# A recurrent unit's elimination matrix fetched through DRAM, and its outputs summed in one PSUM bank

## The chip, the core and the metric

The kernel runs on one core of one Trainium2 chip. The metric is the device time of one launch in microseconds. Engines are named as in the profile: PE (TensorE matmul), PEld (its weight loads), DVE (VectorE), ACT (ScalarE), POOL (GpSimd) and SP, whose queue issues every DMA of this kernel.

## The reference

Two layers of a hybrid block run on 256 latent and 256 context tokens of width 2048. Each layer normalises, projects with `w_in`, runs three branches on the projection's columns (grouped-query attention, a bidirectional RWKV-7 scan, pooling), concatenates and projects with `w_out`. What the change touches is the RWKV branch: 8 heads of size 64, one scan in each direction.

```python
def step(S, inp):
    r_t, w_t, k_t, v_t, kk_t, a_t = inp
    sa = jnp.einsum('bhvk,bhk->bhv', S, kk_t)
    S = S * w_t[:, :, None, :] - sa[..., None] * (kk_t * a_t)[:, :, None, :] + v_t[..., None] * k_t[:, :, None, :]
    return S, jnp.einsum('bhvk,bhk->bhv', S, r_t)
```

The outputs of both directions are added, normalised per head, and gated. Layer 1 needs no output for the context tokens.

## The kernel before, in words

**The main stream.** Weights arrive as 256 KB tiles `wf`; ACT casts each to a rounded high part and DVE subtracts it from the tile (`w_split`, lines 1099 to 1116, tiles `sp`); PE multiplies high and low parts with the activations' parts `h` into PSUM tiles `acc` (`main_in`, `main_out`).

**The recurrent units.** In each layer 8 units, each a pair of heads (group `g`, 0 to 3) by a stream of 256 tokens (`s`, context or latent), are cut into 4 chunks of 64 tokens. Of the 16 units 12 need outputs (`need`): 8 in layer 0, 4 in layer 1. A unit passes through workers that hand it on by queues:

- `front` (line 1297) loads r, k, v, normalises k into `kk`, and makes the factors `W` and `BK` of both directions.
- `back` (line 1413) multiplies them on PE and masks the products on DVE into `UB` and `W`. Then it copies the 32x32 diagonal blocks of the triangular matrices into a tile `N0` (lines 1444 to 1448, eight ACT copies).
- `elim` (line 1457) inverts those blocks. Two DVE transposes (lines 1460 to 1463) spread `N0` into `DT`, the only tile of its class, and 31 steps of one product and one sum each follow on DVE (lines 1469 to 1475), in a chain. Four small transposes give the inverse in two orders, `T1` and `T2`.
- `fin` (line 1486) joins 32-blocks to 64-blocks with copies on ACT and small matmuls.
- `scan` (line 1526) takes 4 steps, in each chunk `i` forward and chunk `3-i` backward. A step's outputs are accumulated by 8 matmuls in a PSUM tile `psO`, which DVE copies or adds into an SBUF tile `OT` (lines 1594 to 1600). After the last step `OT` is normalised (lines 1604 to 1614) and transposed back.

**What sets the order.** The kernel is a program that plans itself: workers yield instructions, and `Scheduler.run` (lines 544 to 625) emits them one by one by a model of the engines, by the time at which each could start and its worker's priority. Every engine then runs its instructions strictly in the order emitted, and waits on semaphores for what they need. A DMA's price in the plan is

```python
            if op.eng == "D":
                self.free_at["D"] = s + 60
                st = max(self.dma_free, s + 60)
                self.dma_free = st + op.dur / 350.0
                end = self.dma_free + DMA_LATENCY
```

with `op.dur` its bytes and `DMA_LATENCY` 2900, all in ns (line 203, lines 589 to 593). `HELD` (line 208, used in line 572) is added to the start of a DVE or ACT instruction whose partitions begin elsewhere than those of the one before it.

**PSUM** has 8 banks of 128x512; tiles of class `scan` may hold up to 3, and 2 are kept for them.

## Time and profile before

| what | value |
|---|---|
| three runs | 1724.2, 1725.89 (median), 1728.25 us |
| profiled execution, its own time | 1729.24 us |
| span of its trace, first to last instruction | 1727.4 us |
| mean granted clock of PE | 0.987 |
| DMA | 349.77 MB, mean 202 GB/s |

The profile lists busy time by engine and by stretch, groups of instructions with a mean duration and the idle time ahead of them, what each engine waited for, the DMAs, and the chain of work that ended last, followed back from the end. A busy PE is not a PE at its peak: matmuls overlap, and a group's mean is the time that one takes from start to end, not the distance between two. Nearly all instructions are emitted by one line, 588, where the planner calls them, so groups are told apart by their tiles: `tp<-dt,tp` is written to a tile `tp` from tiles `dt` and `tp`.

In the span the stretch from 216 to 720 us holds the recurrent units of layer 0, from 720 to 1080 us there are none, and from 1080 to 1620 us those of layer 1.

### The profile page before, as it was taken

What the parts mean: (1) busy time and instruction counts of PE and PEld (TensorE: products, weight loads), DVE (VectorE), ACT (ScalarE), POOL (GpSimd) and SP (SyncE); (2) the same over time, 40 slices, a digit from 0 to 9 for tenths busy, and PEclk for the clock granted to TensorE, in tenths of its full rate; (3) what the DMA queues carried; (4) which work ended last, traced back from release to release, by engine and by line L of the source; (5) the groups of instructions that cost most, each with busy time, mean ns of one, the idle gap of its engine ahead of it and who ended that gap; (6) DMA issues with size and microseconds to landing.
All of it is one profiled execution on the core that took longest, in us unless ns stands there. A gap on an engine that the chain in (4) does not pass through costs nothing.

```text
span 1727.4 us, 38237 instructions
## 1 busy us (share of the span) xinstructions
PE 1657.9 (96%) x13658; PEld 1336.4 (77%) x13658; DVE 1348.7 (78%) x4250; ACT 929.0 (54%) x2279; POOL 9.3 (1%) x77
## 2 busy tenths in 40 slices
PE   4899999999999999999999999989999999999997
PEld 3677676776777777777777889789999988998885
DVE  4335889898898898854557685899999999999663
ACT  5333454544555555534346574666546757766461
POOL 0000000000000000000000000000000000000000
PEclk9999999999999999999999999999999999999998
DMA  9993763567566655568579964574523554564762
GB/s 330 374 364 104 248 198 102 178 205 230 162 190 184 218 186 182 178 205 297 193 238 361 331 214 156 160 259 142 160 87 125 167 152 150 178 186 151 259 199 98
DMA packets 217822, 349.77 MB, mean 202 GB/s; under 512 B 22880, under 2 KB 61856, under 8 KB 217632
## 3 DMA queue, kind: packets, MB, share of 16 engines
q1 hardware_dynamic: 217632, 347.34, 61.4%
q8 instruction: 107, 1.75, 0.4%
q14 instruction: 83, 0.68, 0.1%
HBM read 316.41 MB, written 30.83 MB: 201 GB/s over the span
## 4 chain that ended last, share of the span: by engine, by line
PE 76%; DVE 10%; DMA 9%; ACT 2%; issue 2%; SPq 1%; DVEq 0%; ACTq 0%
PE acc L588 54%; PE pr L588 6%; PE att L588 6%; PE scan L588 5%; PE ada L588 4%; DVE tp L588 3%; DMA wa<-in_ada_w_dram 2%; DVE sp L588 2%; DMA w<-in_ada_w_dram 2%; DMA wf<-in_w_in_dram 2%; DVE rf L588 1%; DMA pw<-in_w_in_dram 1%; DVE dt L588 1%; PE st L588 1%; SPq L588 1%
## 5 line engine op out<-in xcount | busy, mean ns | idle before, releaser
L588 PE MATMUL acc<-h,sp 128*128 128x256 f32 (+1 forms) x5088 | 971.2, 339 | 11.4 <-DVE h L588 4.3
L588 PEld LDWEIGHTS acc<-h,sp 128*128 128x128 f32 x5088 | 759.1, 189 | 124.9 <-issue 11.6
L588 DVE TENSOR_TENSOR sp<-wf,sp 128x512 fp32r<-128x512 f32 (+1 forms) x568 | 359.4, 661 | 38.0 <-ACT sp L588 31.9
L588 ACT CAST sp<-wf 128x512 fp32r<-128x512 f32 (+1 forms) x624 | 351.3, 604 | 21.5 <-PE acc L588 5.7
L588 PE MATMUL acc<-sp,h 128*128 128x512 f32 x1152 | 278.4, 398 | 0.1
L588 PEld LDWEIGHTS acc<-sp,h 128*128 128x128 f32 x1152 | 215.0, 189 | 50.1 <-DVE sp L588 1.0
L588 DVE TENSOR_TENSOR tp<-tp 128x60 f32<-128x60 f32 (+21 forms) x552 | 134.4, 246 | 7.1 <-ACT tp L588 0.3
L588 DVE TENSOR_TENSOR tp<-dt,tp 128x48 f32<-128x48 f32 (+23 forms) x496 | 111.0, 224 | 6.3
L588 PEld LDWEIGHTS scan<-rf 128*64 128x64 f32 x1344 | 57.2, 138 | 34.6 <-issue 9.5
L588 PE MATMUL scan<-rf 128*64 128x64 f32 x1344 | 78.0, 233 | 1.7 <-DVE rf L588 1.0
L588 PE MATMUL ada<-wa,cs 128*2 128x256 f32 x1024 | 71.9, 378 | 2.5 <-DMA wa<-in_ada_w_dram 2.2
L588 ACT CAST pw<-pw 128x512 fp32r<-128x512 f32 x56 | 34.8, 622 | 65.4 <-DMA pw<-in_w_in_dram 59.8
L588 DVE TENSOR_TENSOR rf<-tp 64x256 f32<-64x256 f32 x176 | 69.2, 419 | 0.2
L588 DVE STREAM_TRANSPOSE dt<-tp 128x1024 f32<-128x1024 f32 x32 | 65.8, 2075 | 0.1
L588 DVE TENSOR_TENSOR pw<-pw 128x512 f32<-128x512 f32 x56 | 38.4, 686 | 34.5 <-ACT pw L588 34.2
L588 ACT ACTIVATE aq<-att,q 128x512 f32<-128x512 f32 (+1 forms) x48 | 34.0, 708 | 57.0 <-DVE q L588 40.7
L588 DVE COPY adasb<-ada 2x128 f32<-2x128 f32 (+1 forms) x32 | 11.4, 357 | 66.0 <-ACT adasb L588 63.9
L588 DVE SCALAR_TENSOR_TENSOR q<-q 128x4 f32<-128x4 f32 (+3 forms) x378 | 56.9, 155 | 3.7
L588 PE MATMUL ada<-w,cs 128*2 128x128 f32 x1024 | 37.5, 295 | 21.2 <-DMA w<-in_ada_w_dram 20.2
L588 ACT COPY rf<-scan 64x128 f32<-64x128 f32 x128 | 33.3, 260 | 44.1 <-PE scan L588 40.6
L588 ACT COPY adasb<-ada 2x128 f32<-2x128 f32 (+1 forms) x32 | 9.9, 309 | 87.2 <-PE ada L588 83.7
L588 ACT COPY sm<-scan 128x128 f32<-128x128 f32 x64 | 17.1, 267 | 69.6 <-PE scan L588 69.1
(153 smaller groups left out, 1936.6 us busy)
## 6 DMA issues: line engine op xcount, KB each, us to landing
wf<-in_w_in_dram SPq DMA_DIRECT2D x384, 256.0 KB, 3.6
wa<-in_ada_w_dram SPq DMA_DIRECT2D x256, 256.0 KB, 4.6
wf<-in_w_out_dram SPq DMA_DIRECT2D x192, 256.0 KB, 4.7
w<-in_ada_w_dram SPq DMA_DIRECT2D x128, 256.0 KB, 5.4
pw<-in_w_in_dram SPq DMA_DIRECT2D x56, 256.0 KB, 4.5
w<-pw SPq DMA_DIRECT2D x56, 256.0 KB, 2.5
sp<-w SPq DMA_DIRECT2D x56, 256.0 KB, 3.5
wf<-in_w_in_dram SPq DMA_DIRECT2D x48, 128.0 KB, 4.6
```

The lines of the kernel that those rows point to most:

```text
L588: op.call(**op.args)
```

## The change

It has four parts. First, `kk` is made from `k` directly: ACT's Square takes the scale `rw_k_k`, a `scalar_tensor_tensor` takes it too, and the separate product `kr` is gone. Second, `N0` and the two transposes into `DT` are gone: `back` writes the blocks from `UB` to a DRAM scratch `nd` (4 of them in turn) with 8 DMAs of 16 KB, in runs of 128 B, and `elim` reads them into `DT` with 16 DMAs of 64 KB, each of which repeats 8 KB to 8 partitions. Both directions now lie in `DT` in the same order, so the steps of `elim` address the two directions with access patterns built by hand, and `T1` and `T2` change roles for direction 1. Third, `psO` is one PSUM bank for all 4 steps of a unit, with a column range for each chunk; the copies and sums into `OT` are gone, and the normalisation reads the bank. Fourth, `HELD` is 120.25 in place of 121.75.

```diff
--- before.py
+++ after.py
@@ -205,7 +205,7 @@
 WHOLE = (128, 128)
 SWITCH = 95.0
 BACK = 60.0
-HELD = 121.75
+HELD = 120.25
 HOLD = {None: 1000.0, "ada": 3000.0}
 PRIO = {"setup": 6, "start": 6, "scan": 5, "front": 3, "back": 4, "elim": 4, "fin": 4, "evac": 4, "pre": 4, "gate": 4, "att": 4, "rg": 5, "mix": 5, "load": 1, "ada": 3, "wl": 2, "ws": 6, "main": 0, "norm": 6, "turn": 3, "post": 6}
 
@@ -646,6 +646,7 @@
         self.ahead = AHEAD_OF()
         self.low = {w: [dram("w%d_%d" % (n, i), [128, 512]) for i in range(2)] for n, w in enumerate(self.ahead)}
         self.ygd = [dram("ygd%d" % l, [4, 128, 512]) for l in range(DEPTH)]
+        self.nd = [dram("nd%d" % i, [4, 2, 4, 32, 32]) for i in range(4)]
         self.sch = Scheduler(tiles, CLASSES, log)
         self.sch.set_phase(PHASES["start"])
         self.flags = set()
@@ -1310,15 +1311,13 @@
             yield D_.dma_start(out=rkv[j], in_=self.rkvd[l][j, g, :, cs])
         r, k, v = rkv
 
-        kr = yield Alloc("tp", (128, 256))
-        yield V.tensor_scalar(out=kr, in0=k, scalar1=self.vec(l, "rw_k_k", g), scalar2=None, op0=ALU.mult)
         sq = yield Alloc("tp", (128, 256))
-        yield S.activation(out=sq, in_=kr, func=AF.Square)
+        yield S.activation(out=sq, in_=k, func=AF.Square, scale=self.vec(l, "rw_k_k", g))
         psb = yield from self.norm_bc(sq, self.k("hones"), 1.0, 1e-24, ALU.max, "pr")
         self.free(sq)
         kk = yield Alloc("tp", (128, 256))
-        yield V.tensor_tensor(out=kk, in0=kr, in1=psb[:, 0:256], op=ALU.mult)
-        self.free(kr, psb)
+        yield V.scalar_tensor_tensor(out=kk, in0=k, scalar=self.vec(l, "rw_k_k", g), in1=psb[:, 0:256], op0=ALU.mult, op1=ALU.mult)
+        self.free(psb)
 
         BK, W = [], [[], []]
         yield Until(lambda: len(self.fq) == 0)
@@ -1441,38 +1440,41 @@
                 yield V.tensor_tensor(out=W[p][d][H[1 - p], 0:nj].rearrange("p j c t -> p c j t"),
                                       in0=pa[H[1 - p], :, 0:nj, :], in1=mk(H[1 - p]), op=ALU.mult)
                 self.free(psA[p])
-        N0 = yield Alloc("tp", (128, 2, 4, 32))
-        for q in range(4):
-            b = q % 2
-            for d in range(2):
-                yield S.copy(out=N0[Q[q], d], in_=UB[d][Q[q], :, 0, 32 * b:32 * b + 32])
+        nd = self.nd[self.count.setdefault("nd", 0) % len(self.nd)]
+        self.count["nd"] += 1
+        for d in range(2):
+            for q in range(4):
+                b = q % 2
+                yield D_.dma_start(out=nd[q, d].rearrange("c s t -> s c t"), in_=UB[d][Q[q], :, 0, 32 * b:32 * b + 32])
         for d in range(2):
             psW = yield Alloc("pr", (128, 512))
             for c in range(4):
                 yield T.transpose(out=psW[:, 128 * c:128 * c + 128], in_=BK[d][:, c].rearrange("p a b -> p (a b)"), identity=ident)
             yield S.copy(out=BK[d].rearrange("p c h k -> p (c h k)"), in_=psW)
             self.free(psW)
-        self.push(self.bq, (N0, (l, g, s, need, RS, W, UB, BK, PC, bv)))
-
-    def elim(self, N0, unit):
+        self.push(self.bq, (nd, (l, g, s, need, RS, W, UB, BK, PC, bv)))
+
+    def elim(self, nd, unit):
         V = self.V
         DT = yield Alloc("dt", (128, 2, 32, 32))
-        for d in range(2):
-            src = N0[:, d].rearrange("p c t -> p t c").unsqueeze(2).to_broadcast([128, 32, 8, 4])
-            dst = DT[:, 0].rearrange("p a b -> p b a") if d == 0 else DT[:, 1]
-            yield V.transpose(out=dst, in_=src)
-        self.free(N0)
+        for q in range(4):
+            for c in range(4):
+                src = nd[q, :, c].rearrange("d s t -> d (s t)").unsqueeze(0).to_broadcast([8, 2, 1024])
+                yield self.D.dma_start(out=DT[32 * q + c:32 * q + 32:4].rearrange("p d s t -> p d (s t)"), in_=src)
         ZZ = yield Alloc("tp", (128, 2, 32, 4))
         TM = yield Alloc("tp", (128, 256))
         z0 = self.k("z0").rearrange("p (a m) -> p a m", m=4).unsqueeze(1).to_broadcast([128, 2, 32, 4])
         yield V.tensor_copy(out=ZZ, in_=z0)
+        grid = lambda x, o, *dims: bass.AP(x.tensor, x.offset + o, [list(x.ap[0])] + [list(n) for n in dims])
         for t in range(31, 0, -1):
-            m0 = t // 8
+            r, m0 = 31 - t, t // 8
             M = 4 - m0
             tm = TM[:, 0:2 * t * M].rearrange("p (d a m) -> p d a m", d=2, a=t)
-            yield V.tensor_tensor(out=tm, in0=DT[:, :, 0:t, t:t + 1].to_broadcast([128, 2, t, M]),
-                                  in1=ZZ[:, :, t:t + 1, m0:4].to_broadcast([128, 2, t, M]), op=ALU.mult)
-            yield V.tensor_tensor(out=ZZ[:, :, 0:t, m0:4], in0=ZZ[:, :, 0:t, m0:4], in1=tm, op=ALU.add)
+            n = grid(DT, t, (1024 + 32 * (r + 1) + r - t, 2), (32, t), (0, M))
+            row = grid(ZZ, 4 * t + m0, (128 + 4 * r - 4 * t - m0, 2), (0, t), (1, M))
+            z = grid(ZZ, m0, (128 + 4 * (r + 1) - m0, 2), (4, t), (1, M))
+            yield V.tensor_tensor(out=tm, in0=n, in1=row, op=ALU.mult)
+            yield V.tensor_tensor(out=z, in0=z, in1=tm, op=ALU.add)
         self.free(DT, TM)
         T1 = yield Alloc("tp", (128, 2, 32, 4))
         T2 = yield Alloc("tp", (128, 2, 4, 32))
@@ -1488,14 +1490,14 @@
         for q in range(4):
             b = q % 2
             yield S.copy(out=UB[0][Q[q], :, 0, 32 * b:32 * b + 32], in_=T1[Q[q], 0].rearrange("p c u -> p u c"))
-            yield S.copy(out=UB[1][Q[q], :, 0, 32 * b:32 * b + 32], in_=T2[Q[q], 1])
+            yield S.copy(out=UB[1][Q[q], :, 0, 32 * b:32 * b + 32], in_=T1[Q[q], 1].rearrange("p c u -> p u c"))
         psY = yield Alloc("pr", (128, 512))
         for u in range(4):
             for p in range(2):
                 q0, q1 = Q[2 * p], Q[2 * p + 1]
                 o = slice(32 * u, 32 * u + 32)
                 yield T.matmul(out=psY[q1, o], lhsT=UB[0][q0, u, 0, 32:64], rhs=T2[q0, 0, u, :], start=True, stop=True)
-                yield T.matmul(out=psY[q0, o], lhsT=UB[1][q1, u, 0, 0:32], rhs=T1[q1, 1, :, u], start=True, stop=True)
+                yield T.matmul(out=psY[q0, o], lhsT=UB[1][q1, u, 0, 0:32], rhs=T2[q1, 1, u, :], start=True, stop=True)
         YS = yield Alloc("tp", (128, 4, 32))
         yield S.copy(out=YS.rearrange("p u t -> p (u t)"), in_=psY[:, 0:128])
         self.free(psY)
@@ -1505,7 +1507,7 @@
                 q0, q1 = Q[2 * p], Q[2 * p + 1]
                 o = slice(32 * u, 32 * u + 32)
                 yield T.matmul(out=psZ[q0, o], lhsT=YS[q1, u, :], rhs=T1[q1, 0, :, u], start=True, stop=True)
-                yield T.matmul(out=psZ[q1, o], lhsT=YS[q0, u, :], rhs=T2[q0, 1, u, :], start=True, stop=True)
+                yield T.matmul(out=psZ[q1, o], lhsT=YS[q0, u, :], rhs=T1[q0, 1, :, u], start=True, stop=True)
         psz3 = psZ[:, 0:128].rearrange("p (u t) -> p u t", u=4)
         for p in range(2):
             yield S.copy(out=UB[0][Q[2 * p], :, 0, 32:64], in_=psz3[Q[2 * p]])
@@ -1526,9 +1528,8 @@
     def scan(self, Sc, l, g, s, need, RS, W, UB, W2, PC, bv):
         V, S, G, T, D_ = self.V, self.S, self.G, self.T, self.D
         ident = self.k("ident")
-        OT = None
         if need:
-            OT = yield Alloc("ts", (128, 4, 64))
+            psO = yield Alloc("scan", (128, 512))
         if s == 1:
             for p in range(2):
                 yield V.tensor_copy(out=RS[H[p], p, 0:4:3, :], in_=Sc[H[p]])
@@ -1546,11 +1547,10 @@
             yield S.copy(out=X, in_=psX[:, 0:128])
             self.free(psX)
             if need:
-                psO = yield Alloc("scan", (128, 512))
                 for d in range(2):
                     for p in range(2):
-                        yield T.matmul(out=psO[H[p], 64 * d:64 * d + 64], lhsT=W[p][d][:, 1, c[d], :], rhs=RS[:, p, c[d], :],
-                                       start=(d == 0), stop=False, skip_group_check=True)
+                        yield T.matmul(out=psO[H[p], 64 * c[d]:64 * c[d] + 64], lhsT=W[p][d][:, 1, c[d], :], rhs=RS[:, p, c[d], :],
+                                       start=(i == 0 and d == 0), stop=False, skip_group_check=True)
             psS = yield Alloc("scan", (128, 512))
             for d in range(2):
                 for p in range(2):
@@ -1569,8 +1569,8 @@
             if need:
                 for d in range(2):
                     for p in range(2):
-                        yield T.matmul(out=psO[H[p], 64 * d:64 * d + 64], lhsT=UB[d][H[p], c[d], 1, :], rhs=RS[H[p], p, c[d], :],
-                                       start=False, stop=(d == 1), skip_group_check=True)
+                        yield T.matmul(out=psO[H[p], 64 * c[d]:64 * c[d] + 64], lhsT=UB[d][H[p], c[d], 1, :], rhs=RS[H[p], p, c[d], :],
+                                       start=False, stop=(i == 3 and d == 1), skip_group_check=True)
             if not last:
                 sm = yield Alloc("sm", (128, 2, 64))
                 pn3 = psN[:, 0:128].rearrange("p (d v) -> p d v", d=2)
@@ -1591,20 +1591,16 @@
             else:
                 self.free(Sc)
                 Sc = None
-            if need:
-                po = psO[:, 0:128].rearrange("p (d v) -> p d v", d=2)
-                if i < 2:
-                    yield V.tensor_copy(out=both(OT, c), in_=po)
-                else:
-                    yield V.tensor_tensor(out=both(OT, c), in0=both(OT, c), in1=po, op=ALU.add)
-                self.free(psO)
         self.free(RS, *W[0], *W[1], *UB, *W2, PC)
         if need:
             st = yield Alloc("q", (128, 4))
-            yield V.tensor_reduce(out=st, in_=OT, axis=AX.X, op=ALU.add)
+            O4 = psO[:, 0:256].rearrange("p (c v) -> p c v", c=4)
+            yield V.tensor_reduce(out=st, in_=O4, axis=AX.X, op=ALU.add)
             yield V.tensor_scalar(out=st, in0=st, scalar1=1.0 / 64, scalar2=None, op0=ALU.mult)
             bc = lambda ap: ap.unsqueeze(2).to_broadcast([128, 4, 64])
-            yield V.tensor_tensor(out=OT, in0=OT, in1=bc(st), op=ALU.subtract)
+            OT = yield Alloc("ts", (128, 4, 64))
+            yield V.tensor_tensor(out=OT, in0=O4, in1=bc(st), op=ALU.subtract)
+            self.free(psO)
             sq = yield Alloc("ts", (128, 4, 64))
             yield S.activation(out=sq, in_=OT, func=AF.Square)
             yield V.tensor_reduce(out=st, in_=sq, axis=AX.X, op=ALU.add)
```

## Rows read from the trace of the kernel before

**Rows 1.** The profile page: busy time and share of each engine.

```profile
PE 1657.9 (96%) x13658; PEld 1336.4 (77%) x13658; DVE 1348.7 (78%) x4250; ACT 929.0 (54%) x2279; POOL 9.3 (1%) x77
```

**Rows 2.** Stretches: from:to us, length; busy PE, PEld, DVE, ACT, POOL; clock, DMA share, GB/s.

```profile
216.00:720.00 504.00, 495.89 (x4287) 362.78 (x4286) 455.97 (x1577) 264.42 (x689) 3.81 (x34) 1.00 0.58 185
720.00:1080.00 360.00, 357.41 (x2125) 283.40 (x2124) 223.28 (x509) 186.34 (x399) 0.61 (x4) 1.00 0.74 246
1080.00:1620.00 540.00, 529.76 (x5066) 482.03 (x5065) 501.24 (x1708) 347.45 (x892) 3.53 (x28) 0.99 0.51 163
```

**Rows 3.** Waits of PE from 216 to 1620 us: total us, times, longest.

```profile
PE acc L588 <- DMA sp<-w: 2.3, 2, 1.1
PE ada L588 <- DMA wa<-in_ada_w_dram: 2.2, 4, 0.7
PE acc L588 <- DVE sp L588: 2.1, 4, 1.1
```

**Rows 4.** Chain that ended last: whole run, 216:720 us, 1080:1620 us.

```profile
PE 76%; DVE 10%; DMA 9%; ACT 2%; issue 2%; SPq 1%; DVEq 0%; ACTq 0%
...
by line: PE acc L588 32.3%; PE scan L588 8.7%; PE pr L588 8.4%; PE att L588 8.1%; DVE tp L588 6.8%; PE ada L588 6.6%; DMA wa<-in_ada_w_dram 5.0%; DVE sp L588 4.3%; issue 3.7%; DVE rf L588 3.1%; DVE dt L588 2.1%; DMA rkvd<-ev 1.4%; DVE q L58
...
by line: PE acc L588 58.2%; PE pr L588 9.6%; PE scan L588 7.4%; PE att L588 6.6%; DVE tp L588 3.0%; DMA wf<-in_w_in_dram 2.0%; DMA sp<-w 1.5%; DVE sp L588 1.4%; DVE dt L588 1.3%; DMA x1d<-y 1.1%; issue 1.0%; DVE q L588 0.9%; DVE rf L588 0.8
```

**Rows 5.** One piece of that chain, in order of time: start, us, what.

```profile
949.11 58.03 PE acc L588 x248
```

**Rows 6.** Groups of instructions by shape: count, busy us, mean ns, idle before.

```profile
L588 PE MATMUL acc<-sp,h 128*128 128x512 f32 x1152 | 278.4, 398 | 0.1
...
L588 DVE STREAM_TRANSPOSE dt<-tp 128x1024 f32<-128x1024 f32 x32 | 65.8, 2075 | 0.1
...
L588 ACT COPY tp<-rb 32x128 f32<-32x128 f32 x128 | 37.6, 295 | 20.0 <-DVE rb L588 18.2
...
L588 ACT ACTIVATE tp<-tp 128x256 f32<-128x256 f32 x80 | 30.4, 413 | 30.1 <-DVE tp L588 27.7 <-DVE q L588 1.9
...
L588 DVE TENSOR_REDUCE q<-ts 128x4 f32<-128x256 f32 x24 | 9.8, 409 | 0.1
...
L588 DVE COPY ts<-scan 128x128 f32<-128x128 f32 x24 | 6.8, 281 | 0.7 <-PE scan L588 0.4
L588 DVE TENSOR_TENSOR ts<-ts,scan 128x128 f32<-128x128 f32 x24 | 6.7, 281 | 0.1
...
L588 DVE TENSOR_REDUCE q<-att 128x1 f32<-128x256 f32 x16 | 6.7, 416 | 2.4 <-PE att L588 2.4
...
L588 DVE TENSOR_TENSOR tp<-tp,pr 128x256 f32<-128x256 f32 x16 | 6.6, 414 | 3.1 <-PE pr L588 2.9
...
L588 DVE SCALAR_TENSOR_TENSOR tp<-tp,hk 128x256 f32<-128x256 f32 x12 | 5.7, 476 | 0.0
...
L588 DVE TENSOR_SCALAR tp<-tp,vecs 128x256 f32<-128x256 f32 x16 | 5.5, 342 | 0.6 <-DMA tp<-rkvd 0.6
...
L588 ACT ACTIVATE at<-acc,vecs 128x256 f32<-128x256 f32 x8 | 3.8, 471 | 0.0
```

**Rows 7.** DMA issues on SP in order of time: start, us, what.

```profile
506.55 1.38 SPq L588 DMA_DIRECT2D tp<-rkvd  x3
...
511.43 1.75 SPq L588 DMA_DIRECT2D wa<-in_ada_w_dram  x4
```

**Rows 8.** DMA issues by tile: count, KB each, median us to landing.

```profile
tu<-in_rw_w_up_dram SPq DMA_DIRECT2D x16, 64.0 KB, 3.1
...
ta<-in_pool_w_dram SPq DMA_DIRECT2D x8, 64.0 KB, 4.3
...
gpd<-tl SPq DMA_DIRECT2D x2, 16.0 KB, 2.6
```

**Rows 9.** DVE from 1612 to 1616 us; the bracket is idle time before.

```profile
1613.21 0.48 DVE L588 SCALAR_TENSOR_TENSOR at<-y,vecs,at 128x256 f32<-128x256 f32 x1 [3.62 <-DMA y<-ygd]
```

**Rows 10.** PE in the same stretch.

```profile
1612.29 1.86 PE L588 MATMUL acc<-h,sp 128*128 128x256 f32 x13
```

## The prediction, made before the changed kernel ran

> **What bounds the kernel now.** I read the busy time of the whole run first. PE is busy for 96% of the span and DVE for 78% [rows 1]. By stretch the picture sharpens: while the recurrent units of layer 0 run, PE is busy 495.9 of 504 us and DVE 456.0, which is 90%; in layer 1 they stand at 529.8 and 501.2 of 540 us, so DVE reaches 93%. Between the two, DVE falls to 62% [rows 2]. PE is the bound, DVE a close second, and only where the change works.
>
> A busy PE is not a full one. In the pure stretch of the chain 248 matmuls take 58.03 us, 234 ns each [rows 5], while one of them lasts 398 ns from start to end [rows 6]. So short waits of PE hide inside its busy time, and an idle PE of 8.1 + 10.2 us in the two stretches [rows 2] is no ceiling for a gain. The waits that do show are small, 2.1 us for DVE's weight splits and 4.5 us for two kinds of load [rows 3]. For what a relieved engine is worth I therefore use the chain that ended last: DVE carries 10% of it, DMA 9%, ACT 2%. In layer 0 the tiles `tp`, `sp`, `rf` and `dt` of DVE make 6.8 + 4.3 + 3.1 + 2.1 = 16.3%, in layer 1 `tp`, `sp`, `dt`, `q` and `rf` 3.0 + 1.4 + 1.3 + 0.9 + 0.8 = 7.4% [rows 4].
>
> **What goes.** (1) The two transposes into `DT`: 32 of 2075 ns, 65.8 us of DVE [rows 6]. On the chain they hold 2.1% of 504 us and 1.3% of 540 us, 10.6 + 7.0 = 17.6 us [rows 4]. I count this as the gain: the rest was hidden by PE.
>
> (2) The copies and sums into `OT`: 24 + 24 of 281 ns [rows 6], 13.5 us of DVE, 9.0 in layer 0 and 4.5 in layer 1. At the chain shares above that is worth 1.5 + 0.3 = 1.8 us. The final reduction and subtraction now read PSUM; a reduction of 256 columns takes 416 ns from there and 409 from SBUF [rows 6], so I add nothing. `psO` now holds a bank of class `scan` for the whole unit. In a step the tiles for X, S and N are asked for one after the other, each when the one before is evacuated, and fit in one further bank, which stays kept for them; I take 0. If that cover fails, each step waits once for an evacuation of 281 ns, 48 x 0.28 = 13 us at most.
>
> (3) `kr`: one product of 342 ns goes, and the next, 414 ns, becomes one with a scalar per partition, 476 ns for the nearest shape: 16 x (342 - 62) = 4.5 us of DVE, at about 12% of the chain 0.5 us. ACT's Square with such a scale goes from 413 to at most 471 ns [rows 6], 0.9 us in all, hidden in an ACT that is busy 54% [rows 1].
>
> (4) The 128 copies into `N0`, 295 ns each, 37.6 us of ACT [rows 6], at ACT's 2% of the chain [rows 4] 0.8 us. The steps of `elim` keep their count, sizes and strides; the exchanged roles of `T1` and `T2` keep every count. Both cost 0; an ACT copy or a matmul that reads with the other stride shifts a few tens of ns among 128, under cover of the same idle ACT.
>
> (5) `HELD`: no instruction is priced by it on the chip, only the order shifts. No row prices an order. I take 0, and bound it by the 18.3 us of PE's idle time in the two stretches [rows 2], either way.
>
> Gains: 17.6 + 1.8 + 0.5 + 0.8 = **20.7 us**.
>
> **What comes.** Each unit issues 8 DMAs of 16 KB and 16 of 64 KB on SP, 384 in all, behind which the loads of weights stand in the same queue: `wf`, `wa` and `pw`. Three issues in a row take 1.38 us and four take 1.75 us [rows 7], some 0.45 us each. The planner books 60 ns for an issue, 65536 / 350 = 187 ns for the bytes and 2.9 us to land. So it holds a unit's 16 reads landed 16 x 0.187 + 2.96 = 5.95 us after the first could go. On the chip the last is issued after 15 x 0.45 = 6.75 us and lands 3.1 us later (64 KB loads: 3.1 and 4.3 us [rows 8]), at 9.85 us: **3.9 us after the planned time.** The 8 writes add nothing to this: 16 KB landed in 2.6 us [rows 8] against a planned 2.9, and half of them leave while DVE still masks the other direction.
>
> The first product of `elim` is emitted for the planned time, so DVE would stand there waiting for `DT`, up to 3.9 us a unit, 16 x 3.9 = 62 us, with the splits of weights and the scan's sums queued behind it. What does a late DVE cost PE? At one place the trace shows it: DVE stood 3.62 us before 1613.21 us, waiting for data that had gone through DRAM [rows 9], and PE ran on, with no gap ahead of its matmuls at 1612.29 us [rows 10]. There the price was 0. The other end is the whole 3.9 us. A delay of DVE at a random moment would count by its share of the chain, 16.3% and 7.4%. The wait comes on top of a queue that is 90% full, so I take a fifth, nearer to the row than to the whole: 16 x 3.9 x 0.2 = 12.5 us.
>
> The queue too: 16 issues take 7.2 us where the plan books 3.0, so loads behind them go out 4.2 us late. DMAs named in the two chains hold 5.0 + 1.4 = 6.4% and 2.0 + 1.5 + 1.1 = 4.6% [rows 4]; 8 x 4.2 x (0.064 + 0.046) = 3.7 us. The bounds are 0 and 67 us, but a late load and a late `DT` come in the same burst and are not added at their full size.
>
> Losses: 12.5 + 3.7 = **16.2 us**.
>
> **Sum.** 20.7 - 16.2 = 4.5 us less. The profiled execution took 1729.2 us, so 1724.7 us by its own time. It lies 3.3 us above the median of the three runs; against that median the forecast is **1721.4 us**, with 1712 to 1729 as its own range.
>
> **Rivals.** *A, DVE was the real second bound, 1700 us.* All of the change takes 65.8 + 13.5 + 4.5 = 84 us from DVE. If the order packs PE so much denser that half of it counts, the gain is 42 us and the net 26. For it: DVE at 90% and 93%, and the PE waits hidden in busy time. Against it: PE's visible waits for DVE are 2.1 us.
>
> *B, DVE waits at the first product and PE with it, 1746 us, slower.* The place is the first read of `DT` in each unit; the price is not a fifth but three fifths of 3.9 us, as splits reach PE just in time: 37.4 + 3.7 - 20.7 = 20 us more. It decides once PE's lead over the splits is shorter than DVE's wait. For it: 4.3% of layer 0's chain are splits [rows 4], and the plan knows nothing of the real issue time. Against it: the wait that cost PE nothing [rows 9, 10].
>
> *C, the reads of `DT` use half of the DMA engines, 1756 us, slower.* The outermost dimension of each read has 8 entries. In layer 0 the 16 engines move 185 GB/s at a share of 0.58 [rows 2], 19.9 GB/s for a full one; 8 of them take 6.6 us for a unit's 1 MB, no more than the 7.2 us of issue. But 58% of their time is taken; in the rest it is 15.7 us, 8.5 us later still. A wait of 12.4 us at a fifth costs 40 us, the loads behind it 11 us, against 20.7 us gained. The Trainium skill, page "DMA: Bandwidth & Descriptors", section "Rules for kernel authors", says that an outermost dimension of fewer than 16, such as a leading broadcast, confines a DMA to at most that many engines. No run here shows it yet; if it holds and weights do not give way, C follows, and if the reads find gaps, the sum above stands.
>
> *D, no change, 1726 us.* PE's work is the same to the matmul, and its idle time of 18 us is not DVE's; what the chain passes through, other work takes over, and the lateness is covered as there [rows 9, 10].
>
> **How the numbers follow.** The forecast gets 0.32, A 0.20, B 0.30, C 0.08, D 0.10. A measurement of this kernel tells about 0.2% from no change, 3.5 us. The forecast lies 4.5 us below, so of its 0.32 I put 0.22 to faster, 0.09 to the same and 0.01 to slower. Faster: 0.22 + 0.20 = 0.42. Same: 0.09 + 0.10 = 0.19. Slower: 0.01 + 0.30 + 0.08 = 0.39. The range goes from just below A, 1698, to 1757 us, past B and up to C; beyond it lie a DVE wait that counts whole and an order much better than A's.
>
> **What would show it.** Right: DVE falls from 1349 to about 1265 us and ACT from 929 to about 893; `tp<-dt,tp` shows idle time released by DMA of some 4 us a unit; PE's waits for `sp` stay within some 15 us; issues of the 64 KB reads stand 0.45 us apart. Wrong: no idle time of DVE before `tp<-dt,tp` (then the lateness was misjudged, and A or D holds); reads that land far more than 4 us after issue (C); PE waits for `sp`, `wa` or `scan` grown by 30 us (B). The forecast fails as a whole if PE's spacing in the two stretches changes with the order alone, which nothing above prices.

## The result, and the profile after

The changed kernel took **1867.3 us** (median of four runs, 1863.8 to 1873.8) against 1725.1 us of the kernel before, timed beside it: ratio 1.083, 95% interval 1.079 to 1.086. It is 142 us slower, where 4.5 us less were forecast, and beyond the range, which ended at 1757 us.

The page of the changed kernel, busy time by engine and the engines' shares of the chain that ended last, to be read beside [rows 1, 4]:

```profile
PE 1694.3 (91%) x13658; PEld 1363.4 (73%) x13658; DVE 1288.0 (69%) x4155; ACT 896.8 (48%) x2152; POOL 8.9 (0%) x77
...
PE 65%; DVE 13%; SPq 9%; DMA 8%; ACT 3%; issue 2%; DVEq 0%; ACTq 0%
```

DVE lost 95 instructions and ACT 127, and both are less busy. But PE's share fell from 96% to 91%: of a span of 1865.2 us it stands idle for 170.9, against 69.5 before. SP's queue, 1% of the chain before, holds 9%. The same stretches as [rows 2]:

```profile
216.00:720.00 504.00, 452.01 (x3809) 327.28 (x3807) 379.70 (x1346) 217.03 (x552) 3.56 (x34) 0.93 0.57 179
720.00:1080.00 360.00, 351.89 (x2154) 266.51 (x2154) 221.98 (x574) 173.72 (x382) 0.11 (x1) 0.99 0.73 248
1080.00:1620.00 540.00, 486.62 (x4254) 439.12 (x4254) 428.49 (x1460) 290.98 (x706) 3.83 (x31) 0.94 0.48 152
```

The units now reach beyond 745 and beyond 1640 us. In either stretch of theirs PE has lost over 40 us of busy time, and its granted clock fell from 1.00 and 0.99 to 0.93 and 0.94. Both engines are idler at once, so neither is short of capacity: they wait. The group of the first reader of `DT`, before and after, and the issues of the new DMAs on SP (min, median and max duration in ns):

```profile
L588 DVE TENSOR_TENSOR tp<-dt,tp 128x48 f32<-128x48 f32 (+23 forms) x496 | 111.0, 224 | 6.3
...
L588 DVE TENSOR_TENSOR tp<-dt,tp 128x48 f32<-128x48 f32 (+23 forms) x496 | 111.2, 224 | 125.4 <-DMA dt<-nd 35.9 <-DMA wf<-in_w_in_dram 30.2 <-DMA nd<-rb 21.9
...
L588 SPq DMA_DIRECT2D dt<-nd x256: 643/656/1352, 229.3 to 1634.8; - x128
L588 SPq DMA_DIRECT2D nd<-rb x128: 302/420/1457, 218.3 to 1595.9; - x128
```

119 us more of idle time, 7.4 us for each of 16 units. The group holds all 31 products of a unit, but 118.3 of the 125.4 us stand at the 16 first ones. One unit, on SP and then on DVE, in order of time:

```profile
717.77 6.48 SPq L588 DMA_DIRECT2D dt<-nd  x8
724.30 0.43 SPq L588 DMA_DIRECT2D wf<-in_w_in_dram  x1
724.77 5.57 SPq L588 DMA_DIRECT2D dt<-nd  x8
730.46 0.37 SPq L588 DMA_DIRECT2D w<-pw  x1
730.92 0.39 SPq L588 DMA_DIRECT2D wf<-in_w_in_dram  x1
731.41 1.83 SPq L588 DMA_DIRECT2D wa<-in_ada_w_dram  x4
```

```profile
719.02 0.69 DVE L588 TENSOR_TENSOR sp<-wf,sp 128x512 fp32r<-128x512 f32 x1 [2.94 <-ACT sp L588]
722.74 0.69 DVE L588 TENSOR_TENSOR pw<-pw 128x512 f32<-128x512 f32 x1 [3.03 <-ACT pw L588]
...
724.83 0.69 DVE L588 TENSOR_TENSOR sp<-wf,sp 128x512 fp32r<-128x512 f32 x1
732.64 0.26 DVE L588 TENSOR_TENSOR tp<-dt,tp 128x62 f32<-128x62 f32 x1 [7.12 <-DMA w<-pw]
```

Eight reads in a row take 5.57 us, **0.70 us each**, where [rows 7] gave 0.45 for other loads. The last one's issue ends at 730.34 us and the first product starts 2.30 us later. DVE stands from 725.52 to 732.64. The bracket names another DMA, since the wait is put down to whatever came last by the profile; the SP rows show what it waited for. PE in the same unit, and its clock before, in and behind its own pause:

```profile
731.27 0.45 PE L588 MATMUL scan<-rf,rb 64*64 64x64 f32 x8
738.21 2.56 PE L588 MATMUL ada<-wa,cs 128*2 128x256 f32 x16 [6.49 <-DMA wa<-in_ada_w_dram]
```

```profile
725.00:732.00 7.00, 6.72 (x60) 4.70 (x58) 0.52 (x1) 1.41 (x4) 0.00 (x0) 1.00 0.47 148
732.00:738.00 6.00, 0.00 (x0) 0.00 (x0) 4.77 (x19) 0.00 (x0) 0.00 (x0) 0.82 0.89 288
738.00:745.00 7.00, 6.79 (x42) 3.88 (x43) 5.41 (x23) 1.09 (x3) 0.00 (x0) 0.66 0.37 141
745.00:760.00 15.00, 15.00 (x108) 11.22 (x107) 14.34 (x77) 10.03 (x24) 0.00 (x0) 1.00 0.47 146
```

PE runs on for six microseconds of DVE's wait and then stops itself, here for a load of `wa` that SP could only issue once the sixteen reads were out. After 6.5 us of idleness the clock averages 0.66 over 7 us, between its two levels of 1.2 and 2.4 GHz, and is back at 1.00 in the last row. So a pause is paid for a second time. Elsewhere PE waits for DVE itself; its waits from 216 to 1730 us, beside [rows 3]:

```profile
PE ada L588 <- DMA wa<-in_ada_w_dram: 22.9, 7, 7.1
PE acc L588 <- DVE sp L588: 17.8, 6, 4.9
PE scan L588 <- ACT sm L588: 15.5, 4, 6.4
PE att L588 <- DVE aq L588: 15.4, 4, 7.5
PE att L588 <- DVE q L588: 13.6, 2, 8.2
```

The longest single ones, 7 to 8 us, are as long as DVE's wait, and they fall on whatever PE needed next. The unit shown is no exception: in 15 of the 16 units PE has a pause of 3.9 to 8.2 us, which begins about when DVE comes to a stand or up to 12 us later.

### The profile page after: what moved, and what is told of

Its sections match the earlier page's. It is cut to its first block, busy times and chain, and to the rows that moved or that the text cites. A ratio compares the mean times of both kernels' runs of the same rounds, so it can differ in the third digit from the quotient of the medians.

```text
span 1865.2 us, 38504 instructions
## 1 busy us (share of the span) xinstructions
PE 1694.3 (91%) x13658; PEld 1363.4 (73%) x13658; DVE 1288.0 (69%) x4155; ACT 896.8 (48%) x2152; POOL 8.9 (0%) x77
## 4 chain that ended last, share of the span: by engine, by line
PE 65%; DVE 13%; SPq 9%; DMA 8%; ACT 3%; issue 2%; DVEq 0%; ACTq 0%
PE acc L588 46%; SPq L588 9%; PE att L588 5%; PE scan L588 4%; PE ada L588 4%; DVE tp L588 4%; PE pr L588 4%; DVE rf L588 2%; DVE sp L588 2%; DMA wa<-in_ada_w_dram 2%; DMA w<-in_ada_w_dram 2%; DMA pw<-in_w_in_dram 1%; DMA wf<-in_w_in_dram 1%; DVE q L588 1%; PE st L588 1%
## 5 line engine op out<-in xcount | busy, mean ns | idle before, releaser
L588 PE MATMUL acc<-h,sp 128*128 128x256 f32 (+1 forms) x5088 | 988.4, 343 | 33.1 <-DVE sp L588 13.1
L588 PEld LDWEIGHTS acc<-h,sp 128*128 128x128 f32 x5088 | 776.9, 194 | 148.6 <-DVE sp L588 15.7
L588 DVE TENSOR_TENSOR tp<-dt,tp 128x48 f32<-128x48 f32 (+23 forms) x496 | 111.2, 224 | 125.4 <-DMA dt<-nd 35.9
L588 PE MATMUL ada<-wa,cs 128*2 128x256 f32 x1024 | 80.1, 396 | 23.5 <-DMA wa<-in_ada_w_dram 23.3
L588 ACT CAST pw<-pw 128x512 fp32r<-128x512 f32 x56 | 34.7, 620 | 94.8 <-DMA pw<-in_w_in_dram 82.5
L588 PEld LDWEIGHTS ada<-wa,cs 128*2 128x2 f32 x1024 | 22.4, 84 | 59.1 <-DMA wa<-in_ada_w_dram 30.1
L588 ACT COPY rf<-pr 64x128 f32<-64x128 f32 (+1 forms) x96 | 34.7, 369 | 51.2 <-PE pr L588 48.5
L588 ACT COPY rf<-scan 64x128 f32<-64x128 f32 x128 | 33.2, 259 | 52.9 <-PE scan L588 50.1
L588 ACT ACTIVATE at<-acc 128x512 f32<-128x512 f32 (+1 forms) x84 | 38.5, 500 | 35.5 <-PE acc L588 30.9
```

Source lines behind the costliest of these rows:

```text
L588: op.call(**op.args)
```

## The experiments

Three suspects stood behind one picture: DVE's wait at the first product (the theory), SP's queue, which is blocked for as long (rival Q), and the order that `HELD` and the kept bank bring (rivals P and O). Each run is timed beside the kernel before.

**Which part.** First the change without its DRAM part, then the DRAM part alone:

```diff
-        nd = self.nd[self.count.setdefault("nd", 0) % len(self.nd)]
+        N0 = yield Alloc("tp", (128, 2, 4, 32))
...
+            yield V.transpose(out=dst, in_=src)
```

> The DRAM part undone (N0 and the two transposes back); one bank for psO, the fused kr and HELD = 120.25 stay. Theory (the loss lies in the reads of DT alone): 1715 to 1730 us, ratio to before 0.994 to 1.003, PE's idle time near the 70 us of before. Rival P (the bank that psO keeps for a whole unit, or the order that HELD gives, costs it): over 1750 us, with PE's waits in scan and sp as in the changed kernel.

```diff
-HELD = 120.25
+HELD = 121.75
...
-            psO = yield Alloc("scan", (128, 512))
+            OT = yield Alloc("ts", (128, 4, 64))
```

> The kernel before with the DRAM part alone (HELD = 121.75). Theory: the whole loss, 1850 to 1885 us, with DVE idle some 100 to 125 us in front of the 496 products tp<-dt,tp. Rival P: under 1800 us, since the bank and HELD are as before.

Measured: 1733.6 us (1.0042, interval 1.0024 to 1.0059) and 1878.5 us (1.0889, 1.0861 to 1.0918). The first is 0.4% slower than before, a little over its expectation; the whole of the large loss lies in the DRAM part, with DVE idle for 124.6 us at the first products. Rival P falls as an explanation of it.

**DVE's wait or SP's queue.** The reads of `DT` moved to GpSimd's queue, and, apart from that, the planner told what an issue costs:

```diff
+        self.DP = Engine("D", nc.gpsimd)
...
-                yield self.D.dma_start(out=DT[32 * q + c:32 * q + 32:4]...
+                yield self.DP.dma_start(out=DT[32 * q + c:32 * q + 32:4]...
```

> The changed kernel with the 256 reads of DT issued from GpSimd's queue, the order of all else unchanged. Theory (DVE's wait is the loss): the reads still take their time to issue there, DVE's idle time in front of tp<-dt,tp stays over 80 us, and the time stays over 1820 us. Rival Q (SP's queue blocked): the loads on SP go out 11 us earlier in each unit, PE's wait for wa (23 us) and ACT's for pw go, and the time falls under 1780 us.

```diff
-                self.free_at["D"] = s + 60
-                st = max(self.dma_free, s + 60)
+                cost = {"dt": 700, "nd": 430}.get(op.writes[0].tensor.name.split("_")[0].rstrip("0123456789"), 60)
+                self.free_at["D"] = s + cost
+                st = max(self.dma_free, s + cost)
...
-            for c in range(4):
+            for c in range(3, -1, -1):
...
-HELD = 120.25
+HELD = 120.5
```

> The changed kernel, with the planner told 700 ns for each issue of a read of DT and 430 ns for each write of nd, and the four reads of a quadrant in the reverse order (so that the last read is the one that the planner sees the first product wait for); HELD = 120.5. Instructions, bytes and issue times stay as they are. Theory (DVE stands at the first product because the order was made for an earlier DT): DVE has other work meanwhile, its idle time in front of tp<-dt,tp falls from 111 us to under 40 us, and the time to 1740 to 1790 us. Rival Q (the 180 us of SP's queue are the loss, through late loads): the time stays over 1820 us whatever DVE does. Rival R (the bandwidth of the reads is the loss): the same, over 1820 us, with the reads landing late after their issue.

From GpSimd's queue: 1856.3 us (1.0757, 1.0735 to 1.0779). DVE's group, PE's wait for `wa`, and the issues there:

```profile
L588 DVE TENSOR_TENSOR tp<-dt,tp 128x48 f32<-128x48 f32 (+23 forms) x496 | 111.2, 224 | 114.3 <-DMA dt<-nd 107.1
...
PE ada L588 <- DMA wa<-in_ada_w_dram: 4.0, 6, 1.8
...
L588 POOL DMA_DIRECT2D dt<-nd x256: 551/551/788, 228.6 to 1625.9; - x128
```

With SP free the wait for `wa` went, as rival Q said, and the time fell only 11.0 us, just by what DVE's idle time fell (125.4 to 114.3). PE's pause moved to other operands, and PE still stands idle for 160.5 us: the two waits lay side by side, and taking away one left the other. The Trainium skill, page "DMA: Bandwidth & Descriptors", section "Rules for kernel authors", says that spreading DMAs over several issuing engines brings no bandwidth and only saves the issuing sequencer's time; the run agrees, with 0.55 us an issue in place of 0.66 and DVE's wait nearly as long. What the shorter issues saved was lost behind them: the first product starts 3.7 us after the end of the last issue, 2.3 in the changed kernel, and 14.2 us after the first issue began, 14.1 in the changed kernel (medians of the 16 units).

With the price told, and the four reads of a quadrant in reverse: 1757.1 us (1.0192, 1.0160 to 1.0224). SP still issues 256 reads at a median of 656 ns, but the planner gave DVE other work first:

```profile
L588 DVE TENSOR_TENSOR tp<-dt,tp 128x48 f32<-128x48 f32 (+23 forms) x496 | 111.1, 224 | 25.0 <-DMA dt<-nd 8.6 <-DMA nd<-rb 3.7 <-DMA wf<-in_w_in_dram 3.2
```

110 of the 142 us are gone with the wait, at the same instructions, bytes and issue times. Rivals Q and R expected over 1820. (The 111 us in the expectation is the group's busy time; its idle time had been 125.4.) The order is another one here, so this run alone doesn't part the wait from the order.

**Issue or bytes.** `nd` laid out so that one read fills a quadrant:

```diff
-            for c in range(4):
-                src = nd[q, :, c].rearrange("d s t -> d (s t)").unsqueeze(0).to_broadcast([8, 2, 1024])
-                yield self.D.dma_start(out=DT[32 * q + c:32 * q + 32:4]...
+            src = nd[q].rearrange("c d s t -> c (d s t)").unsqueeze(0).to_broadcast([8, 4, 2048])
+            yield self.D.dma_start(out=DT[32 * q:32 * q + 32].rearrange("p d s t -> p (d s t)"), in_=src)
```

> The changed kernel with nd laid out by quadrant and chunk, so that one read of 256 KB fills a quadrant of DT: 4 reads a unit in place of 16, the same bytes, the planner's prices as they were. Theory (each issue holds SP's queue 0.70 us, and DVE's wait is issue time): 12 x 0.70 = 8.4 us less of issue a unit, DVE's idle time in front of tp<-dt,tp falls from 125 us to under 60, and the time to 1735 to 1790 us. Rival S (issue time goes by bytes or by descriptors, not by transfer): four issues take some 2.6 us each, and the time stays over 1840 us. Rival R (the transfer itself is slow, 1 MB on 8 of 16 engines): issues are short but the reads land 7 to 16 us after them, DVE's idle time there stays over 90 us, and the time over 1820 us.

Measured: 1791.5 us (1.0373, 1.0353 to 1.0393), just over the theory's bound, as is DVE's idle time of 63.5 us against 60. A unit's issues, DVE's first product, and DVE's group:

```profile
698.30 3.33 SPq L588 DMA_DIRECT2D dt<-nd  x4
```

```profile
708.42 0.26 DVE L588 TENSOR_TENSOR tp<-dt,tp 128x62 f32<-128x62 f32 x1 [3.71 <-DMA dt<-nd]
...
L588 DVE TENSOR_TENSOR tp<-dt,tp 128x48 f32<-128x48 f32 (+23 forms) x496 | 111.6, 225 | 63.5 <-DMA dt<-nd 45.5 <-DMA sp<-w 4.9 <-DMA wf<-in_w_out_dram 3.3
```

A read of 256 KB is issued in 655 ns, as one of 64 KB is, so issue time goes by transfer, and rival S falls. But now the bytes show: the last issue ends at 701.63 us, and the data are there 6.8 us later instead of 2.3. Sixteen issues had hidden a slow transfer behind them. From the first issue to the first product it takes 11.0 us with four reads and 14.1 with sixteen (medians of the 16 units), so of the 8.4 us of issue saved only 3 came back. Half of rival R was right.

**The same order, without the wait.** All runs so far but the GpSimd one changed the order too. These two keep the changed kernel's order instruction for instruction, but send only one or eight plain reads of weights into `DT`, without broadcast or a wait for `nd`, so the units invert weights in place of their own blocks:

```diff
-            op.call(**op.args)
+            if op.eng != "D" or not op.writes[0].tensor.name.startswith("dt"):
+                op.call(**op.args)
+            else:
+                self.plain(op, 1, 16)
...
+        if j % (per // n) == 0:
+            j = j // (per // n) * k
+            op.call(out=self.whole[...][j:j + k]..., in_=self.weights[j:j + k])
```

> The changed kernel, planned and ordered instruction for instruction as it is, but of the 16 reads of DT that a unit issues only one is sent, a plain read of 1 MB of weights into the whole of DT, with no broadcast and no wait for nd; the recurrent units' outputs are then not those of the reference. Only when DT is there and SP's 15 issues change, the order does not. Theory (the loss of 142 us is DVE standing at the first product, at about 1 us for each): the idle time there falls under 20 us and the time to 1720 to 1755 us. Rival O (the order that HELD = 120.25 gives is what is bad, DVE's wait only what shows of it): over 1800 us with that idle time gone.

```diff
-                self.plain(op, 1, 16)
+                self.plain(op, 8, 16)
```

> As the run above, with 8 plain reads of 128 KB each a unit in place of 16 of 64 KB, the last of them at the place of the fifteenth. DT is then late by part of what it is in the changed kernel. Theory: the time above that of the run with one read is 0.9 to 1.3 times the growth of DVE's idle time in front of tp<-dt,tp. Rival O: no such proportion, over 1800 us in both.

Measured: 1741.4 us (1.0095, 1.0072 to 1.0119) and 1809.0 us (1.0494, 1.0464 to 1.0525). The unit shown above, on DVE, in the run with one read, then its page row, then the group in both runs:

```profile
661.87 0.69 DVE L596 TENSOR_TENSOR pw<-pw 128x512 f32<-128x512 f32 x1 [2.69 <-ACT pw L596]
...
663.96 0.69 DVE L596 TENSOR_TENSOR sp<-wf,sp 128x512 fp32r<-128x512 f32 x1
664.57 0.27 DVE L596 TENSOR_TENSOR tp<-dt,tp 128x62 f32<-128x62 f32 x1
...
PE 1658.0 (95%) x13658; PEld 1337.5 (77%) x13658; DVE 1285.1 (74%) x4155; ACT 896.6 (52%) x2152; POOL 8.9 (1%) x77
...
L596 DVE TENSOR_TENSOR tp<-dt,tp 128x48 f32<-128x48 f32 (+23 forms) x496 | 111.1, 224 | 12.7 <-DMA dt<-in_w_in_dram 5.5
```

```profile
L596 DVE TENSOR_TENSOR tp<-dt,tp 128x48 f32<-128x48 f32 (+23 forms) x496 | 111.1, 224 | 72.5 <-DMA wf<-in_w_in_dram 22.6 <-DMA nd<-rb 13.4 <-DMA wa<-in_ada_w_dram 13.3
```

The same work in the same order, and no gap. At 12.7, 72.5 and 125.4 us of idle time the order takes 1741.4, 1809.0 and 1867.3 us: 67.6 us for the first 59.8 and 58.2 for the next 52.9, **1.1 us for each us that DVE stands at the first product**, over the whole length. The spans differ by 127.3 us between the ends (1865.2 and 1737.9); 91.0 of these are PE idle, and 36.3 the same 13658 matmuls busy for longer, at a clock of 0.951 against 0.985. That is how the price comes out above 1. The steps do free SP along with DVE; that SP alone is not the cause rests on the GpSimd run. They also drop the reads' wait for the writes of `nd`, which is short: the first read is issued 0.8 us after the last write's issue has ended, and 0.6 us in the run with one read (medians of the 16 units).

Then the other way round, the wait kept and the order changed:

```diff
-HELD = 120.25
+HELD = 121.75
```

> The changed kernel with HELD = 121.75. Theory: 1850 to 1885 us, another order with the same wait, DVE idle 105 to 125 us at the first products. Rival O: 1760 to 1830 us, since HELD = 120.25 then carries a good part of the loss.

Measured: 1859.3 us (1.0779, 1.0748 to 1.0810) with 118.0 us of idle time. The line through the three runs gives 1741.4 + 1.12 x (118.0 - 12.7) = 1859.3. It gives 1855 for the GpSimd queue (measured 1856.3), 1755 for the priced reads (1757.1), 1798 for four reads (1791.5) and 1867 for the DRAM part alone (1878.5). These orders differ, and an order alone is worth up to 27 us below, so part of the close fit is luck; the same line gives 1740 for a run below that took 1772.4. Rival O falls as an explanation of the large loss.

**The small parts.** The bank and `kr` together, the bank alone, `kr` alone, and `HELD` alone, each on the kernel before:

```diff
-        yield V.tensor_scalar(out=kr, in0=k, scalar1=self.vec(l, "rw_k_k", g), scalar2=None, op0=ALU.mult)
...
+            psO = yield Alloc("scan", (128, 512))
```

> The kernel before with the one bank for psO and the fused kr alone, HELD = 121.75 as before. The first experiment (these two with HELD = 120.25) took 0.4% longer than before. Theory: these two give the 2.3 us of the prediction, HELD's order cost the 0.4%: 1718 to 1727 us, ratio 0.996 to 1.001. Rival P (the bank kept for a unit makes the scan wait): 1729 to 1740 us, ratio over 1.002, PE's waits in scan grown.

```diff
-            OT = yield Alloc("ts", (128, 4, 64))
+            psO = yield Alloc("scan", (128, 512))
```

> The kernel before with psO's one bank alone, HELD = 121.75. Prediction's step 2: 1.8 us less, ratio 0.999, at worst 13 us more (1.008) if X, S and N then wait for the one bank that is left. Theory after the run with both: the bank costs what that run lost, ratio 1.002 to 1.005, and kr nothing. Rival K: the ratio stays within 0.999 to 1.001, and the 0.27% belongs to kr.

```diff
-        yield V.tensor_scalar(out=kr, in0=k, scalar1=self.vec(l, "rw_k_k", g), scalar2=None, op0=ALU.mult)
+            yield V.scalar_tensor_tensor(out=kk, in0=k, scalar=...
```

> The kernel before with the fused kr alone, HELD = 121.75. The bank and kr together measured 1.0027, the bank alone 1.0052. Theory (parts off PE's path are worth nothing by themselves, what is measured is the order that they bring along, some per mille either way): ratio 0.995 to 1.003, no nearer to the 0.9997 of the prediction than chance. Rival (4.5 us less of DVE is worth its share, and kr gives what the two runs differ by): ratio 0.996 to 0.999, a version that beats both kernels.

```diff
-HELD = 121.75
+HELD = 120.25
```

> The kernel before with HELD = 120.25 and nothing else. Prediction's step 5: 0, at most 18.3 us either way. Theory: the order is another one, and its effect is that of chance: ratio 0.997 to 1.011, with DVE's and PE's busy time unchanged to 5 us. Rival: HELD = 120.25 belongs to the change and suits it alone; here it costs over 1%.

| on the kernel before | us | ratio, interval |
|---|---|---|
| bank and `kr` | 1730.2 | 1.0027 (1.0014 to 1.0039) |
| bank | 1733.0 | 1.0052 (1.0036 to 1.0068) |
| `kr` | 1727.4 | 1.0007 (0.9995 to 1.0019) |
| `HELD` | 1741.8 | 1.0105 (1.0089 to 1.0121) |

None is a gain. Bank and `kr` together missed the theory's 0.996 to 1.001 and lie where rival P put them. `HELD` alone, with not one instruction added or removed, costs 16.6 us. Both expectations for that run allowed it, but that 120.25 suits the change does not hold: with the change it is the slower value too, 1867.3 against 1859.3 us. The parts don't add up (bank and `kr` take less than the bank alone), as one expects where each also draws another order. Whether the bank's 0.5% is a wait for the class `scan` or its order stays open: PE's waits in `scan` grew from 2.0 to 6.6 us there, half of it one wait of 3.3 us.

**Can it pay once nobody waits?** Four reads, with the planner told 740 ns an issue and 4.5 us more to land, first with all parts and `HELD` = 121.75, then with the DRAM part alone and 120.25:

```diff
+                dt = op.writes[0].tensor.name.startswith("dt")
+                cost = 740 if dt else 60
...
+                end = self.dma_free + DMA_LATENCY + (4500 if dt else 0)
```

> All parts of the change, with four reads of 256 KB a unit, and the planner told what the run before showed: 740 ns for each issue of a read, and 4.5 us more until it has landed; HELD = 121.75 as before. Theory (what is lost is DVE standing at the first product, at a price of about 1 us for each us of it): DVE's idle time in front of tp<-dt,tp falls under 25 us and the time to 1722 to 1745 us, ratio 0.998 to 1.011. Rival A (DVE was a second bound, and the 84 us taken from it show once nobody waits): under 1715 us. Rival R (8 of 16 DMA engines for a burst of 1 MB delay the weights behind it): over 1750 us, PE waiting for wa, wf or sp by over 20 us.

> The kernel before with the DRAM part alone, in the form of the run above (four reads, priced), HELD = 120.25. Theory: DVE idle under 25 us in front of tp<-dt,tp, 1720 to 1750 us. Rival A: under 1715 us. Rival R: over 1750 us with waits of PE for weights.

Then all parts with the change's own `HELD`, and that order with one plain read in place of the four:

```diff
-HELD = 121.75
+HELD = 120.25
```

> All parts of the change with four priced reads, as the run that took 1745 us, with the change's own HELD = 120.25. Theory (with DVE's wait gone, what is left of the loss is the order and some 10 us of weights that land late): 1730 to 1752 us. Rival A (the 84 us taken from DVE show in a better order): under 1722 us.

```diff
-                op.call(**op.args)
+                self.plain(op, 1, 4)
```

> The kernel of the run that took 1772 us (four priced reads, HELD = 120.25), planned and ordered as it is, but with one plain read of 1 MB of weights in place of the four reads that broadcast; outputs not those of the reference. Theory (that run's 46 us over before are its order, as HELD = 120.25 alone cost before 17 us): it stays at 1760 to 1778 us. Rival R (the broadcast reads on half of the DMA engines delay the weights): 1735 to 1755 us, with PE's waits for wa (12 us) and sp (5 us) gone.

| four priced reads | us | ratio, interval | DVE idle at the first products |
|---|---|---|---|
| all parts, 121.75 | 1745.1 | 1.0120 (1.0106 to 1.0134) | 11.1 |
| DRAM part alone, 120.25 | 1741.3 | 1.0097 (1.0081 to 1.0113) | 13.9 |
| all parts, 120.25 | 1772.4 | 1.0260 (1.0246 to 1.0273) | 11.3 |
| the same order, one plain read | 1757.1 | 1.0189 (1.0162 to 1.0217) | 6.6 |

DVE's wait is all but gone in all four, and none beats the kernel before. The first lies on the edge of its expectation. The third missed its own by 20 us: it lies 27 us above the first, by nothing but `HELD`. The fourth, meant to tell order from transfers, came out between the two expectations. Against the kernel before, timed beside each, 45 us became 33: some 13 us go with the broadcast reads, 33 stay with the order. PE's wait for `wa` fell from 11.8 to 2.6 us, that for `sp` did not fall (5.2 and 6.3). So over a quarter of that run's excess went with the reads, and the rest is its order; which instructions the order puts badly was not traced.

No version beats the kernel before.

## Why the prediction was wrong

- **The issue time, the first term of "What comes".** I took 0.45 us an issue from [rows 7], from loads of another form. The reads take 0.70. With 15 x 0.70 + 0.66 + 2.3 = 13.5 us, `DT` comes 7.5 us after the planned 5.95, not 3.9. In the trace the first product starts 14.1 us after the first issue began (median of the 16 units). The landing, 3.0 us from issue, was as taken from [rows 8]. The sum of the waits was 119 us, not 62. A right issue time would not have been all: with a quarter of the issues it still took 11.0 us.
- **The price of a late DVE, one fifth.** This is the step that failed most. It measured 1.1. The row that I leaned on [rows 9, 10] shows one wait near the end, where PE had work queued that needed nothing new from DVE. In a unit PE lives on what DVE gives it (`sp`, `aq`, `q`, and `sm` by way of ACT), in an order fixed beforehand, so it stops too, 6.2 us after DVE in the unit shown, and in that unit the clock drops. The whole wait, which I had set as the end of the bounds, was still below the price.
- **The gains, 20.7 us.** With `DT` in time and all parts in, the changed kernel's order takes 1741.4 us, what `HELD` alone takes with none of them (1741.8). The 17.6 us that the transposes held of the chain came back as nothing that shows. A share of the chain says where the time passed, not what is had by removing it: PE has the same 13658 matmuls, and takes 1658 us of busy time for them either way. That answers rival A for the orders tried: none is faster than the kernel before, but since an order alone moves the time by up to 27 us, A's 26 us in some better order are not ruled out.
- **DVE's busy time, "about 1265 us".** It fell to 1288.0. The groups that went are the ones counted, and the durations of all DVE instructions add up to 82.5 us less (1592.5 before, 1510.0 after). But the page counts overlapping instructions once, and its figure fell by 60.7.
- **Step 2, the bank.** Some 8 us slower by itself instead of 1.8 faster, inside the bound of 13. **Step 3, `kr`:** 0.5 us less forecast, 0.07% more measured, with an interval that holds both. **Step 4, ACT:** 896.8 us against 893: right; what that is worth no run tells.
- **Step 5, `HELD`.** I took 0 with a bound of 18.3 us; by itself it is 16.6 us on the bad side, near that bound; beside other parts it was 3 us, which the noise covers, 8 and 27, each time on the bad side. In the forecast's last sentence the order was named as what nothing priced.
- **SP's queue, 3.7 us.** Nothing of its own shows: with the reads off SP the time fell by what DVE's wait fell.
- **The rivals.** B had the mechanism and the place: DVE at the first product and PE with it. Its sign was there too: PE's waits for `wa`, `sp` and in `scan` stand at 22.9, 17.8 and 15.5 us in the rows above, 2 us each before. It was short in both factors, 37 us in place of 126. C's slow transfer is there, but hidden behind the issues, so nothing of its own shows in this kernel, and it came out only with four reads. D fell with the sum.

With 0.70 us, a price of 1.1 and no gain the same working would have given 16 x 7.5 x 1.1 = 132 us, and with `HELD`'s 17 it would have stood some 7 us above what was measured. That is hindsight: both figures come from these runs.

## What to carry to other kernels

Before moving work from an engine to DMAs, take the issue time from DMAs of the same form, count one queue's issues in a row, and ask what the planner believes of them: an order that expected its data 7 us too early lost more here (126 us) than all the work taken from DVE (some 83 us of instructions). Count the transfer as well: with a quarter of the issues, the same bytes still came 11.0 us after the first one. When an in-order engine stands, count the whole wait and more, unless the trace shows for that very place that the bound engine has work without it. And measure what another order alone does (17 and 27 us here) before reading a gain or a loss of that size as a part's own.

## What the runs showed of the hardware

- The issue of a DMA on SP goes by its form, not its size: medians of 656 and 655 ns for broadcast reads of 64 and 256 KB, 420 for writes of 16 KB, 422 for plain reads of 128 KB and 424 for one of 1 MB. Whether it is the step of zero in the source, the number of dimensions, the source itself, or the number of DMA engines that the next point is about was not separated.
- A plain read of 1 MB landed 6.2 us after its issue (median of 16); by four broadcast reads the data of the unit shown were there 10.1 us after the first issue began. The packets point to how many DMA engines worked. Those of 8 KB, nearly all from the four broadcast reads, stand most often at eight at a time: for 77 of the 160 us in which any is under way, and at more than eight for 5. Those of 4 KB of the one plain read stand most often at sixteen (20 of 68 us). The Trainium skill, page "DMA: Bandwidth & Descriptors", section "Rules for kernel authors", confines a DMA whose outermost dimension has 8 entries to 8 of the 16 engines. The trace agrees with it, by the eight and sixteen packets at a time.
- PE's pauses are paid for again in the clock: in the unit shown 6.5 us of idleness went with a granted clock of 0.66 over the next 7 us. Over the run the same matmuls in the same order took 36 us more of busy time at a mean clock of 0.951 than in the run with one plain read, at 0.985.
